# Output projection summed over three branches beside the DeltaNet, the input embedding inside the mixer, and three small edits

## The chip, the cores and the metric

The kernel runs on one core of a Trainium2 chip. The metric is the time of one execution on the device in microseconds (us); before the change it is 4006.65, the median of three runs (3999.32 to 4006.66). The engines are TensorE (PE, with PEld for its weight loads), VectorE (DVE), ScalarE (ACT), GpSimd (POOL) and SyncE (SP), which here issues every transfer.

## The reference

Two layers run over 512 positions of width 1024. Each layer: a norm, one input projection into four branches of 256 columns (retention A, a gated linear recurrence B, a diagonal state-space model C, a gated DeltaNet D), a norm of each branch, one output projection added to the residual h; then PEER (a top-k choice among 16384 single-neuron experts), added to h; then an embedding of the layer's own input p, times a gate, added to h.

```
def reference(x, p, positions, ...):
    h = x
    for l in range(DEPTH):                      # 2
        z = rmsnorm(h, mix_norm[l])
        (rq, rk, rv, rg, lg, lx, su, dqkv, db, da, dg) = jnp.split(z @ w_in[l], IN_SPLITS, axis=-1)
        y_ret, y_lru, y_s5, y_gdn = retention(...), rglru(...), s5(...), gated_deltanet(...)
        groups = (y_ret, y_lru, y_s5, y_gdn)
        mixed = jnp.concatenate([rmsnorm(y, branch_norm[l, j]) for j, y in enumerate(groups)], axis=-1)
        h = h + mixed @ w_out[l]
        h = h + peer(rmsnorm(h, ffn_norm[l]), peer_wq[l], peer_subkeys[l], peer_u[l], peer_v[l])
        gate = jax.nn.sigmoid(rmsnorm(h, ple_norm[l]) @ ple_wg[l])
        h = h + (p[l] @ ple_wp[l]) * gate
    return rmsnorm(h, final_norm)
```

## The kernel before

All of it is float32. The large products run as three matmuls of two parts each (`group3`): a tensor is split into a rounded high part (`split`: a cast on ACT) and the rest (a subtraction on DVE, or on POOL where `lo_eng` says so). Tokens lie in four blocks of 128 (`tb`), the 1024 columns of h in eight of 128 (`kd`).

In a layer, `mixer` streams `w_in` through `proj` and starts the DeltaNet D (`gen_D`) beside it; then, in the *middle* of the mixer, branches C, A and B run beside D. `self.mix` takes steps from several generators in turn by weights (RC, RA, ...); a scheduler sets from these steps, when the program is built, the fixed order of every engine, and each engine then works strictly in that order. PSUM is shared by banks: `bj` (tiles ps_j) for the branches, `bd` (ps_d) for D, `rbank` (ps_r) for the output projection.

D needs, for each of four token blocks and two pairs of heads, the inverse of two unit lower triangular matrices of 64x64 (`inverse`): a first level that POOL builds with a masked product (Tm) and the addition of the identity to X = (Tm, Mm), then five levels of two small matmul pairs, a masked product and a subtraction on DVE, and a transposition on PE copied back by ACT. Then `state` carries a state through the chunks: a chain of small matmuls and DVE steps, eight chunks long. `rsqrt` of 32 and 16 numbers per partition (drs for D, ars for A) is a power on POOL.

The finished branches lie in zm (a high and a low tile for each branch). `residual` is the output projection: `proj` over four blocks of 256 columns (tiles ps_r), of which the first two begin with the first six of the eight `kd` (`early=6`) while D runs. As each block of columns ends, DVE adds it to h, and `z_cols` prepares the norm that follows for the block before: four squares (zsq, ACT), and for each `kd` four transpositions (ps_t), zhi (ACT) and zlo (DVE). The next product, ps_q of PEER, reads zhi and zlo of all eight `kd`. h is loaded from memory (`open_h`, eight transfers on SP) into space that earlier tiles of the mixer hold till then.

`ple` is the gate stage: it loads p and ple_wp, splits them on ACT and POOL (tiles ph, pl, wph, wpl), and for each block of 256 columns and each `tb` takes 24 matmuls of the gate (ps_g), a tanh, six matmuls of the embedding (ps_q from wph, wpl) and two DVE steps into h. SP's queue is one for all: a transfer that has to wait holds up those behind it, such as the loads of s5t, which branch C reads. Line 347 is `mm`, 351 the subtraction of `split`, 344 `act`, 323 `rsqrt`, 335 `add`.

Of the kernel before, what the change touches and what calls it, by code (L numbers as in the profile page):

```python
# [12 lines left out]
I32 = mybir.dt.int32  # L13
# [53 lines left out]
def consts():  # L67
# [13 lines left out]
    f.add("nlv", -np.stack([lv[0], lv[0].T], 1).astype(np.float32))  # L81
    f.add("lvT", np.stack([m.T for m in lv[1:]], 1))
# [160 lines left out]
class Ker:  # L243
# [191 lines left out]
    def proj(self, z, wap, blocks, pool, bank, wmax=256, lo_eng=None, per=2, early=0):  # L435

# [30 lines left out]
        begun = {}  # L467
        if early:
            for i in range(2):
                for j in range(NTB):  # L470
                    n = blocks[i][1]
                    if i == 0:
                        begun[j] = bank()
                    ps = begun[j][:, i * n : (i + 1) * n]
                    zs = slice(j * P, (j + 1) * P)
                    for kd in range(early):
                        hi, lo = sp[2 * i + kd // 4]
                        zh, zl = z.at(kd)
                        self.group3(ps, zh[:, zs], zl[:, zs], hi[:, kd % 4, :n], lo[:, kd % 4, :n], kd == 0 and i == 0, False)
                    if j == NTB - 1:  # L480
                        for x in ((2, 3), (4,))[i]:
                            spl(x)
                    yield
        for j in begun:
            zs = slice(j * P, (j + 1) * P)
            for i in range(2):
                n = blocks[i][1]
                ps = begun[j][:, i * n : (i + 1) * n]
                for kd in range(early, KD):
                    hi, lo = sp[2 * i + kd // 4]  # L490
                    zh, zl = z.at(kd)
# [1480 lines left out]
```

## Time and profile before

| | |
|---|---|
| median of three runs | 4006.65 us |
| the profiled execution, on the device | 4006.07 us |
| its span, first to last instruction | 4004.0 us |
| mean granted clock of TensorE | 0.987 of full speed |
| PE, DVE, ACT, POOL busy | 97%, 72%, 38%, 16% |
| mixer, layer 0 (input projection, middle, output projection) | about 0 to 196, 196 to 300, 300 to 399 us |
| gate stage, layer 0 | about 1939 to 2020 us |
| mixer, layer 1 | about 2020 to 2196, 2196 to 2300, 2300 to 2368 us |
| gate stage, layer 1, and the last norm | about 3932 to 4004 us |

The rest, some 1500 us in each layer, is PEER. The times of stages are read from the first and the last instruction on their tiles. [...]

### The profile page before, as it was taken

The numbers are of one execution on the slowest core, as the hardware profiler recorded it, in microseconds if no ns is written. First come the engines' busy times: TensorE is split into PE (matmuls) and PEld (weight loads), VectorE is DVE, ScalarE is ACT, GpSimd is POOL, SyncE is SP. The second block draws the span as 40 slices with busy tenths as digits, with TensorE's granted clock in tenths as the row PEclk, the third lists the DMA queues.
The fourth block names the chain that finished last, engine by engine and source line by source line (L and its number), as shares of the span: only waits on it lengthen the run. The fifth ranks groups of instructions, "written<-read, shape, count | busy, mean of one in ns | idle before, by whom it ended". The sixth has DMA issues, their size and how long they took to land. (4 is left out here: it accounts for less than half of the span.)

```text
span 4004.0 us, 54147 instructions
## 1 busy us (share of the span) xinstructions
PE 3893.6 (97%) x20616; PEld 3231.0 (81%) x20616; DVE 2891.9 (72%) x5821; ACT 1512.0 (38%) x2173; POOL 621.5 (16%) x526
## 2 busy tenths in 40 slices
PE   7989999999999999999999899999899999999999
PEld 6768888878888888888898687777788888888888
DVE  9675899968888666555565769998588865555554
ACT  4344255652233233222443443566322232222223
POOL 4441000010002222222132310000100012222221
PEclk9989999999999999999999899999999999999999
DMA  4213254675653444333121133556756533333322
GB/s 146 83 29 106 75 200 176 241 268 187 202 169 122 139 137 150 124 118 109 48 99 45 41 122 110 188 203 244 238 182 201 160 110 127 112 120 118 124 79 85
DMA packets 306981, 554.06 MB, mean 138 GB/s; under 512 B 17696, under 2 KB 196000, under 8 KB 301344
## 3 DMA queue, kind: packets, MB, share of 16 engines
q1 hardware_dynamic: 306720, 550.60, 41.1%
q8 instruction: 162, 2.65, 0.3%
q14 instruction: 99, 0.81, 0.1%
HBM read 439.90 MB, written 110.63 MB: 137 GB/s over the span
## 5 line engine op out<-in xcount | busy, mean ns | idle before, releaser
L1670 DVE TENSOR_TENSOR h<-h,ps_v 128x512 f32<-128x512 f32 x1024 | 677.5, 681 | 627.5 <-PE ps_v L347 626.1
L347 PE MATMUL ps_v<-vhi,whi 128*128 128x512 f32 x2048 | 800.9, 391 | 20.7 <-ACT whi L350 20.3
L347 PE MATMUL ps_u<-zhi,ulo 128*128 128x512 f32 x2048 | 813.0, 397 | 0.5 <-DVE ulo L351 0.5
L347 PE MATMUL ps_u<-zhi,uhi 128*128 128x512 f32 x2048 | 809.9, 395 | 0.4 <-ACT aout L344 0.4
L347 PE MATMUL ps_u<-zlo,uhi 128*128 128x512 f32 x2048 | 808.2, 395 | 0.0
L347 PE MATMUL ps_v<-vlo,whi 128*128 128x512 f32 x2048 | 800.7, 391 | 0.0
L347 PE MATMUL ps_v<-vhi,wlo 128*128 128x512 f32 x2048 | 796.6, 389 | 0.0
L351 POOL TENSOR_TENSOR ulo<-uraw,uhi 128x1024 fp32r<-128x1024 f32 x136 | 328.7, 2417 | 2195.3 <-ACT uhi L350 1602.1
L350 ACT CAST uhi<-uraw 128x1024 fp32r<-128x1024 f32 x256 | 269.8, 1054 | 850.4 <-PE ps_u L347 572.0
L347 PEld LDWEIGHTS ps_v<-vhi,whi 128*128 128x128 f32 x2048 | 385.9, 188 | 104.7 <-ACT whi L350 21.2
L350 ACT CAST whi<-dact 128x512 fp32r<-128x512 f32 x256 | 158.5, 620 | 819.2 <-issue 378.7
L347 PEld LDWEIGHTS ps_u<-zhi,ulo 128*128 128x128 f32 x2048 | 384.9, 188 | 84.0 <-DVE ulo L351 1.4
L347 PEld LDWEIGHTS ps_u<-zlo,uhi 128*128 128x128 f32 x2048 | 385.0, 188 | 83.5
L347 PEld LDWEIGHTS ps_u<-zhi,uhi 128*128 128x128 f32 x2048 | 384.9, 188 | 82.9 <-ACT aout L344 1.2
L347 PEld LDWEIGHTS ps_v<-vlo,whi 128*128 128x128 f32 x2048 | 385.9, 188 | 81.2
L347 PEld LDWEIGHTS ps_v<-vhi,wlo 128*128 128x128 f32 x2048 | 385.2, 188 | 81.5
L332 DVE TENSOR_TENSOR dact<-dact,dg 128x512 f32<-128x512 f32 x256 | 320.6, 1256 | 34.5 <-ACT dact L344 17.1
L351 DVE TENSOR_TENSOR vlo<-vraw,vhi 128x1024 fp32r<-128x1024 f32 x256 | 311.5, 1235 | 26.0 <-ACT vhi L350 26.0
L344 ACT ACTIVATE tstg<-ps_g 128x512 f32<-128x512 f32 x256 | 264.3, 1157 | 128.3 <-PE ps_g L347 126.2
L350 ACT CAST vhi<-vraw 128x1024 fp32r<-128x1024 f32 x256 | 261.8, 1049 | 21.8 <-PE ps_v L347 20.2
L351 DVE TENSOR_TENSOR wlo<-dact,whi 128x512 fp32r<-128x512 f32 x256 | 180.8, 708 | 36.7 <-ACT whi L350 23.6
L329 DVE TENSOR_TENSOR to<-t_iota,tii 128x1024 f16<-128x1024 bf16 x256 | 172.0, 682 | 2.0 <-ACT tii L344 1.7
(467 smaller groups left out, 5410.3 us busy)
## 6 DMA issues: line engine op xcount, KB each, us to landing
uraw<-in_uT_dram SPq DMA_DIRECT2D x256, 512.0 KB, 3.5
vraw<-in_v_dram SPq DMA_DIRECT2D x256, 512.0 KB, 3.8
Gd<-tstg SPq DMA_DIRECT2D x32, 2048.0 KB, 7.0
dg<-Gd SPq DMA_DIRECT2D x64, 1024.0 KB, 6.0
Ad<-aout SPq DMA_DIRECT2D x120, 256.0 KB, 2.1
dact<-Ad SPq DMA_DIRECT2D x120, 256.0 KB, 3.4
wraw<-in_w_in_dram SPq DMA_DIRECT2D x40, 512.0 KB, 3.5
wraw<-in_w_out_dram SPq DMA_DIRECT2D x16, 512.0 KB, 3.6
```

The costliest lines, as they stand in the source:

```text
L329: (eng or self.V).tensor_tensor(out, a, b, op=op)
L332: (eng or self.V).tensor_tensor(out, a, b, op=ALU.mult)
L344: self.A.activation(out, x, f, **k)
L347: self.PE.matmul(out, l, r, start=start, stop=stop)
L350: self.A.copy(hi, x)
L351: (lo_eng or self.V).tensor_tensor(lo, x, hi.bitcast(F32), op=ALU.subtract)
L1670: self.reached = V.tensor_tensor(self.h[:, tb, ds], self.h[:, tb, ds], ps, op=ALU.add).ins
```

## The change

1. Output projection. `residual` goes; `out_early` sums, for two halves of 512 columns, the products of the three branches A, B and C (kd 0 to 5), taken in steps beside D (weight RE = 3). The first half goes to SBUF (`part`, four ACT copies), the second stays in PSUM (`held`). `out_late`, after D, adds `part` to h, then D's two kd to each half and token block, adds each to h, and calls `z_cols` once the last token block of a half is done. So 768 matmuls of 256 columns become 384 of 512.
2. Embedding. p @ ple_wp is no longer computed in `ple`, but in `gen_embed`, taken beside C, A, B and D (weight RA). Its splits go to ACT and DVE; the product is written to memory (Pd) and read back as emb by `ple`. pT and ple_wp pass through the buffer ak of branch A.
3. Residual. The pools of the mixer are laid out in another sequence, and some small tiles of D and A go into another pool, so that the space of h is free sooner.
4. Small edits: `rsqrt` of 16 or more numbers on DVE (a first guess and three Newton steps, ten operations); the first level of `inverse` without POOL's product and addition, as a DVE subtraction and one more transposition (`turned`); the factor lam as two ACT operations in place of one on POOL.

```diff
 def rsqrt(self, pool, out, x, n, tag):
-        self.G.tensor_tensor(out, x, self.mhalf.to_broadcast([P, n]), op=ALU.pow)
+        V = self.V
+        if n < 16:
+            self.G.tensor_tensor(out, x, self.mhalf.to_broadcast([P, n]), op=ALU.pow)
+            return
+        y = out
+        t = pool.tile([P, n], F32, name="rsq_t", tag=tag + "t")
+        V.tensor_scalar(y.bitcast(I32), x.bitcast(I32), -0.5, 1597463007.0, op0=ALU.mult, op1=ALU.add)
+        for _ in range(3):
+            V.tensor_tensor(t, y, y, op=ALU.mult)
+            V.scalar_tensor_tensor(t, t, -0.5, x, op0=ALU.mult, op1=ALU.mult)
+            V.scalar_tensor_tensor(y, t, 1.5, y, op0=ALU.add, op1=ALU.mult)
...
         def inverse(tb, hp):
-            self.mul(lam, m2(low), la2, G)
+            for h in range(2):
+                self.act(lam[:, h], low, AF.Copy, scale=la[:, tb, 2 * hp + h : 2 * hp + h + 1])
...
-            self.mul(Tm, Lm, m2(c("nlv")[:, 0]), G)
...
-            self.mul(Mm, h2(ps[:, 0:256]), m2(c("nlv")[:, 1]))
+            AT = pool.tile([P, 2, P], F32, name="dAT", tag="dAT", bufs=4)
+            self.mul(AT, h2(ps[:, 0:256]), m2(c("lvT")[:, 0]))
             self.mul(aT, h2(ps[:, 256:512]), m2(c("tri")))
-            self.add(X, X, self.ident.unsqueeze(1).unsqueeze(1).to_broadcast([P, 2, 2, P]), G)
+            self.sub(Mm, m2(self.ident), AT)
+            yield
+            def turned():
+                ps = bank()
+                for h in range(2):
+                    self.PE.transpose(ps[:, h * P : (h + 1) * P], Mm[:, h, :], self.ident)
+                self.act(fl(Tm), ps[:, 0:256], AF.Copy)
+            turned()
...
 def mixer(...):
-            self.a_alloc(mx)
             self.b_alloc(mx)
             self.c_alloc(mx)
+            self.mix_alloc(mx)
+            self.d_alloc(mx)
+            self.a_alloc(mx)
...
-                self.mix([(upto(C, "c_half"), self.RC), (a_(), self.RA), (b_(), self.RA), (upto(D, "d_half"), 1)])
+                W = self.gen_embed(l, self.pool(c1, "em", sa), bj, Pd)
+                self.mix([(upto(C, "c_half"), self.RC), (a_(), self.RA), (b_(), self.RA), (W, self.RA), (upto(D, "d_half"), 1)])
...
-            pj = self.residual(self.zm, self.ap["w_out"][l], wp)
+            pj = self.out_early(self.zm, self.ap["w_out"][l], wp)
...
-                self.take(pj, 8)
+                self.mix([(pj, self.RE), (D, 1)])
                 drain((D, 1))
...
-                self.blockwise(pj, znew, gain, banks(...), wp, 0)
+                self.out_late(self.zm, znew, gain, banks(...), wp)
...
+    def out_early(self, z, wap, pool):
...
+        for hf in range(2):
+            b = [self.rbank() for _ in range(NTB)]
+            for c in range(3):
+                spl(3 * hf + c + 1)
...
+                for tb in range(NTB):
+                    self.out_mm(z, b[tb], hf, c, tb, c == 0, hf == 0 and c == 2)
+                    yield
+            if hf == 0:
+                for tb in range(NTB):
+                    self.act(self.part[:, tb, :], b[tb], AF.Copy)
+        self.held = b
...
+    def out_mm(self, z, ps, hf, c, tb, first, last):
+        hi, lo = self.late_w[hf, c]
+        ts = slice(tb * P, (tb + 1) * P)
+        for k in range(2):
+            zh, zl = z.at(2 * c + k)
+            self.group3(ps, zh[:, ts], zl[:, ts], hi[:, k], lo[:, k], first and k == 0, last and k == 1)
+    def out_late(self, z, znew, gain, bank, pool):
...
+            self.add(hs, hs, self.part[:, tb, :])
+        for tbs in ((0, 1, 2), (3,)):
+            for hf in (1, 0):
+                for tb in tbs:
+                    ps = self.held[tb] if hf else self.rbank()
+                    self.out_mm(z, ps, hf, 3, tb, hf == 0, True)
+                    hs = self.h[:, tb, cs[hf]]
+                    self.add(hs, hs, ps)
+                if tbs == (3,):
+                    for i in (2 * hf, 2 * hf + 1):
+                        self.z_cols(znew, gain, i, bank, pool)
...
+    def gen_embed(self, l, pool, bank, Pd):
...
+        nc.sync.dma_start(praw, self.ap["pT"][l].rearrange("(k p) t -> p k t", p=P))
+        parts = [self.zm.at(6 + k) for k in range(2)]
+        for k in range(2):
+            self.split(*parts[k], praw[:, k])
...
+        for i in range(4):
+            wh, wl = (pool.tile([P, 2, 256], F32R, name=n, tag=n) for n in ("wph", "wpl"))
+            self.split(wh, wl, raw(i))
+            load(i + 2)
...
+                        self.group3(ps[:, o : o + 256], ph[:, ts], pl[:, ts], wh[:, k], wl[:, k], k == 0, k == 1)
+                e = self.av[:, t0 : t0 + 2, :]
+                self.act(fl(e), ps, AF.Copy)
+                nc.sync.dma_start(Pd[:, t0 : t0 + 2, 256 * i : 256 * i + 256], e)
...
 def ple(...):
-                    p2 = bq()
-                    for k in range(2):
-                        self.group3(p2[:, 0:256], ph[:, k, ts], pl[:, k, ts], wh[:, k, cs], wl[:, k, cs], k == 0, k == 1)
-                    self.stt(tg, tg, 1.0, p2[:, 0:256], ALU.add, ALU.mult)
+                    self.stt(tg, tg, 1.0, emb[i][:, tb], ALU.add, ALU.mult)
...
-            self.split(ph, pl, praw, self.G)
-            self.split(wh, wl, wraw, self.G)
```

Places in the engines' fixed order. PE, layer 0, middle of the mixer, before: aq and sx are transposed for branches A and C, s5t and xb are products of C and B, ps_d is D.

```order
L347 MATMUL ps_d<-dX,cb 128x256
L1032 MATMUL ps_j<-ca,aq 128x128 x2
L347 MATMUL ps_d<-dX,cb 128x256
L1032 MATMUL ps_j<-ca,aq 128x128
L347 MATMUL ps_j<-s5t_2296,sx_2322 128x256
L1032 MATMUL ps_j<-ca,aq 128x128 x4
L347 MATMUL ps_j<-xb,lruw 128x512
L347 MATMUL ps_d<-dX,cb 128x256 x2
L347 MATMUL ps_d<-dS,dwT 64x128
L347 MATMUL ps_d<-dkT 128x128 x2
```

The same place after; wph, wpl and zm are the parts of ple_wp and of p.

```order
L687 MATMUL ps_d<-ca,dX 128x128 x2
L360 MATMUL ps_d<-dX,dE 128x128 x2
L360 MATMUL ps_d<-dAT,dX 128x128 x4
L1015 MATMUL ps_j<-ca,aq 128x128
L360 MATMUL ps_j<-wph,zm_2433 128x256
L360 MATMUL ps_j<-wpl,zm_2433 128x256
L360 MATMUL ps_j<-wph,zm_2434 128x256
...
L1241 MATMUL ps_j<-ca,sx_2343 128x128
L1015 MATMUL ps_j<-ca,aq 128x128
L1241 MATMUL ps_j<-ca,sx_2343 128x128
L360 MATMUL ps_d<-dAT,dX 128x128 x2
```

Blocks of twelve matmuls of the embedding now stand between those of D and the branches.

SP, layer 0, at the end of the input projection, before: Td is the prepared state space of branch C, s5t its reload.

```order
L448 DMA wraw<-in_w_in_dram 128x4x256 x2
L1095 DMA Td_65<-s5p_1027 128x2048
L448 DMA wraw<-in_w_in_dram 128x4x256 x5
L1062 DMA s5t_2297<-Td_65 128x2560
L1062 DMA s5t_2299<-Td_65 128x1024
L1062 DMA s5t_2301<-Td_65 128x2048
L1062 DMA s5t_2303<-Td_65 128x8
L1067 DMA s5t_2296<-Td_65 32x4x512 x4
L1221 DMA gluw<-in_glu_w_dram 128x2x512
```

After:

```order
L1078 DMA Td_65<-s5p_1022 128x2048
L460 DMA wraw<-in_w_in_dram 128x4x256
L1905 DMA ak<-in_pT_dram 128x2x512
L1916 DMA ak<-in_ple_wp_dram 128x2x256
L1045 DMA s5t_2315<-Td_65 128x2560
L1045 DMA s5t_2317<-Td_65 128x1024
L1045 DMA s5t_2319<-Td_65 128x2048
L1045 DMA s5t_2321<-Td_65 128x8
L1050 DMA s5t_2314<-Td_65 32x4x512 x4
L1204 DMA gluw<-in_glu_w_dram 128x2x512
L937 DMA lruw<-in_lru_w_dram 128x512
L1916 DMA ak<-in_ple_wp_dram 128x2x256 x2
```

pT and a first part of ple_wp have moved ahead of s5t; the second uses the buffer that the first has left.

PE, layer 0, end of the output projection, before (zm is D's and the other branches' parts; ps_t is a transposition of h):

```order
L347 MATMUL ps_r<-whi,zm_3105 128x256
L347 MATMUL ps_r<-wlo,zm_3105 128x256
L347 MATMUL ps_r<-whi,zm_3106 128x256
L364 MATMUL ps_t<-ca,h 128x128 x8
L347 MATMUL ps_q<-zhi,whi 128x512
L347 MATMUL ps_q<-zlo,whi 128x512
L347 MATMUL ps_q<-zhi,wlo 128x512
```

After:

```order
L360 MATMUL ps_r<-whi,zm_2433 128x512
L360 MATMUL ps_r<-wlo,zm_2433 128x512
L360 MATMUL ps_r<-whi,zm_2434 128x512
L377 MATMUL ps_t<-ca,h 128x128 x4
...
L360 MATMUL ps_r<-whi,zm_2433 128x512
L360 MATMUL ps_r<-wlo,zm_2433 128x512
L360 MATMUL ps_r<-whi,zm_2434 128x512
L377 MATMUL ps_t<-ca,h 128x128 x16
L360 MATMUL ps_q<-zhi,whi 128x512 x4
L377 MATMUL ps_t<-ca,h 128x128 x4
L360 MATMUL ps_q<-zlo,whi 128x512
L360 MATMUL ps_q<-zhi,wlo 128x512
```

Before, eight transpositions lie between the last ps_r and ps_q; now sixteen stand between the last ps_r and the first ps_q, and eight more among the first ps_q.

ACT, layer 0, behind D's last piece of zm, before:

```order
L344 ACTIVATE zm_3105<-ps_d,gv 128x128 x2
L344 ACTIVATE zsq,zss<-h 128x256
L350 CAST whi<-wraw 128x1024
L344 ACTIVATE zsq,zss<-h 128x256
L350 CAST whi<-wraw 128x1024
L344 ACTIVATE zsq,zss<-h 128x256 x6
L344 ACTIVATE zhi<-ps_t,gv 128x512 x2
L350 CAST whi<-wraw 128x1024
L344 ACTIVATE zsq,zss<-h 128x256
L350 CAST whi<-wraw 128x1024
L344 ACTIVATE zsq,zss<-h 128x256
```

After:

```order
L357 ACTIVATE zm_2433<-ps_d,gv 128x128 x2
L357 ACTIVATE zsq,zss<-h 128x256 x5
L363 CAST whi<-wraw 128x1024
L357 ACTIVATE zsq,zss<-h 128x256
L363 CAST whi<-wraw 128x1024
L357 ACTIVATE zsq,zss<-h 128x256
L357 ACTIVATE zhi<-ps_t,gv 128x512 x2
L357 ACTIVATE zsq,zss<-h 128x256 x3
L363 CAST whi<-wraw 128x1024
L357 ACTIVATE zsq,zss<-h 128x256
L357 ACTIVATE zhi<-ps_t,gv 128x512
L357 ACTIVATE zsq,zss<-h 128x256
```

The items are the same in kind; in the new order sixteen zsq and eight zhi follow D's last piece with 30 ps_r on PE beside them, where 204 of half the width were beside them before.

## Rows read from the trace of the kernel before

**Rows 1.** The page, first section: engines' busy time, share of span, instructions.
```profile
PE 3893.6 (97%) x20616; PEld 3231.0 (81%) x20616; DVE 2891.9 (72%) x5821; ACT 1512.0 (38%) x2173; POOL 621.5 (16%) x526
```

**Rows 2.** The chain that ended last: start us, us, engine, tile, line, matmuls.
```profile
2359.80 8.27 PE ps_r L347 x69
2382.98 31.73 PE ps_q L347 x136
3272.23 5.48 PE ps_v L347 x24
3969.05 4.19 PE ps_g L347 x35
```

**Rows 3.** Stretches of both mixers: length, engines' busy us, PEclk, DMA share, GB/s.
```profile
196.00:282.00 86.00, 66.11 (x358) 54.55 (x359) 66.17 (x126) 38.00 (x83) 40.28 (x31) 0.80 0.14 40
2196.00:2275.00 79.00, 59.99 (x325) 48.07 (x324) 67.89 (x127) 37.01 (x73) 38.01 (x32) 0.85 0.20 61
240.00:260.00 20.00, 11.35 (x58) 9.62 (x58) 20.00 (x26) 5.06 (x6) 15.70 (x11) 0.70 0.00 1
```

**Rows 4.** PE in layer 0, by time: start, us, line, tiles, [idle before <-releaser].
```profile
192.13 1.95 PE L347 MATMUL ps_d<-dAT,dX 128*128 128x128 f32 x16
202.32 3.62 PE L347 MATMUL ps_d<-dAT,dX 128*128 128x128 f32 x16
250.76 1.22 PE L347 MATMUL ps_d<-dkT 64*128 64x128 f32 x4 [7.37 <-DVE dE L332]
```

**Rows 5.** Instructions by line and form: count, busy us, mean ns, idle before.
```profile
L347 PE MATMUL ps_q<-wph,ph 128*128 128x256 f32 x64 | 18.0, 284 | 0.0
L323 POOL TENSOR_TENSOR drs<-dss,mhalf 128x32 f32<-128x32 f32 x2 | 11.0, 5476 | 1.7 <-DVE dss L638 1.7
L335 POOL TENSOR_TENSOR dX<-dX,ca 128x512 f32<-128x512 f32 x16 | 20.9, 1325 | 4.6 <-DVE dX L332 3.2 <-DVE daT L332 1.3
L351 DVE TENSOR_TENSOR wlo<-dact,whi 128x512 fp32r<-128x512 f32 x256 | 180.8, 708 | 36.7 <-ACT whi L350 23.6 <-PE ps_v L347 2.5
```

**Rows 6.** The gate's start in both layers, by time: start us, us, engine, line.
```profile
1947.90 4.54 POOL L351 TENSOR_TENSOR wpl<-wpraw,wph 128x2048 fp32r<-128x2048 f32 x1
1947.97 4.50 DVE L412 TENSOR_SCALAR zrsh<-zrs 128x4 f32<-128x4 f32 x1 [0.54 <-POOL zrs L323]
3940.06 0.17 DVE L412 TENSOR_SCALAR zrsh<-zrs 128x4 f32<-128x4 f32 x1 [0.40 <-POOL zrs L323]
```

**Rows 7.** Stretches of the gate's start, columns as in rows 3.
```profile
1950.00:1955.00 5.00, 1.55 (x13) 1.56 (x14) 4.19 (x6) 0.69 (x1) 2.44 (x1) 0.98 0.01 3
1955.00:1960.00 5.00, 5.00 (x32) 5.00 (x32) 2.50 (x3) 2.32 (x3) 0.00 (x0) 0.68 0.14 46
3935.00:3940.00 5.00, 4.09 (x32) 3.64 (x31) 3.85 (x5) 3.87 (x6) 0.98 (x1) 1.00 0.31 104
```

**Rows 8.** Stretches of the output projection, columns as in rows 3.
```profile
340.00:372.00 32.00, 28.13 (x192) 21.95 (x190) 16.33 (x54) 10.67 (x31) 5.51 (x10) 0.98 0.11 37
372.00:400.00 28.00, 27.96 (x226) 27.78 (x227) 18.94 (x31) 18.85 (x47) 1.37 (x8) 0.96 0.74 259
2320.00:2380.00 60.00, 59.10 (x437) 54.50 (x436) 32.49 (x67) 27.84 (x67) 10.59 (x52) 1.00 0.46 150
```

**Rows 9.** Behind the output projection, by line and form; columns as in rows 5.
```profile
L344 ACT ACTIVATE zhi<-ps_t,gv 128x512 fp32r<-128x512 f32 x40 | 26.2, 685 | 21.1 <-PE ps_t L364 21.1
L344 ACT ACTIVATE zsq<-h 128x256 f32<-128x256 f32 x48 | 20.0, 417 | 27.9 <-DVE h L341 13.0 <-DVE h L335 12.6 <-ACT zsq L344 1.1
L344 ACT ACTIVATION_READ_ACCUMULATOR zsq<-h 128x1 f32 x48 | 9.1, 189 | 0.0
L350 ACT CAST whi<-wraw 128x1024 fp32r<-128x1024 f32 x88 | 91.7, 1045 | 109.4 <-PE ps_j L347 29.7 <-PE ps_q L347 29.2 <-DMA wraw<-in_w_in_dram 12.7
L335 DVE TENSOR_TENSOR h<-h,ps_r 128x256 f32<-128x256 f32 x32 | 12.6, 416 | 13.7 <-PE ps_r L347 11.1 <-DMA h<-in_x_dram 2.0 <-DMA h<-Hd 0.3
```

**Rows 10.** One issue of the DMA list: KB each, median us to landing.
```profile
praw<-in_pT_dram SPq DMA_DIRECT2D x2, 512.0 KB, 3.9
```

More of the change, by code (lines that the diff above doesn't have):

```diff
@@ L611, in gen_D @@
         yield
[L612 removed]
+        S = self.dS
         V.memset(S, 0.0)
@@ L851, in a_alloc @@
         self.ag = pool.tile([P, NTB, 256], F32, name="ag")
+        self.am = [pool.tile([P, 4, 32], F32, name="am%d" % i) for i in range(2)]
     def a_cons(self, what):
@@ L1828, in take, with load, spl @@
             next(g, None)
-    def residual(self, z, wap, pool):
-        def cons(i):
-            def f(tb, ps):
-                hs = self.h[:, tb, 256 * i : 256 * i + 256]
-                self.add(hs, hs, ps[:, 0:256])
-            return f
-        return self.proj(z, wap, [(256 * i, 256, "T", cons(i)) for i in range(4)], pool, lambda: self.rbank(), per=4, early=6)
+    def out_early(self, z, wap, pool):
+        nc = self.nc
+        seq = [(0, 0), (0, 1), (0, 2), (1, 0), (1, 1), (1, 2), (0, 3), (1, 3)]
+        raws, w = {}, {}
+        self.part = pool.tile([P, NTB, 512], F32, name="part")
+        def load(x):
+            if x < len(seq):
+                hf, c = seq[x]
+                raws[x] = pool.tile([P, 2, 512], F32, name="wraw", tag="wraw", bufs=2)
+                nc.sync.dma_start(raws[x], wap[256 * c : 256 * c + 256, 512 * hf : 512 * hf + 512].rearrange("(k p) c -> p k c", p=P))
+        def spl(x):
+            if x < len(seq):
+                hf, c = seq[x]
+                tag = lambda n: dict(name=n, tag=n if c < 3 else n + str(hf), bufs=2 if c < 3 else 1)
+                w[hf, c] = [pool.tile([P, 2, 512], F32R, **tag(n)) for n in ("whi", "wlo")]
+                self.split(*w[hf, c], raws.pop(x))
+                load(x + 2)
+        load(0)
+        load(1)
+        yield
+        spl(0)
+        yield
+        self.late_w = w
+        for hf in range(2):
+            b = [self.rbank() for _ in range(NTB)]
+            for c in range(3):
+                spl(3 * hf + c + 1)
+                if c == 2 and hf == 1:
+                    spl(7)
+                for tb in range(NTB):
+                    self.out_mm(z, b[tb], hf, c, tb, c == 0, hf == 0 and c == 2)
+                    yield
+            if hf == 0:
+                for tb in range(NTB):
+                    self.act(self.part[:, tb, :], b[tb], AF.Copy)
+        self.held = b
+        yield
@@ L1937, in run @@
             last = l == L - 1
-            self.ple(l, zs[a], None if last else zs[b], None if last else self.gain("mixg", l + 1), out)
+            self.ple(l, zs[a], None if last else zs[b], None if last else self.gain("mixg", l + 1), out, Pd)
             if not last:
```

135 lines of the change are left out of this document (62 added, 73 removed).

## The prediction

> **What bounds the kernel now.** The first section of the page says that TensorE (PE) is busy for 97% of the span [rows 1], and the chain of waits is nearly all matmuls. So a microsecond counts if it takes matmuls off a stretch where PE is full, or puts matmuls where PE stands idle. The chain gives the prices. A matmul of 256 columns takes 4.19 / 35 = 0.120 us (gate, ps_g) and 8.27 / 69 = 0.120 (output projection, ps_r). One of 512 columns takes 5.48 / 24 = 0.228 to 31.73 / 136 = 0.233 us [rows 2]. The table of stretches then shows where PE is not full: in both mixers, in the stage where the branches A, B, C and the DeltaNet D run side by side. [...] Sixteen small matmuls of an inverse take 1.95 us at 192 us and 3.62 at 202, the two levels of the clock, and one wait of 7.37 us there is for DVE [rows 4]. From 240 to 260 us DVE has no free time and PE works 11.35 of 20 us [rows 3]. The output projection and the gate are otherwise full: 27.96 of 28 us in layer 0's last stretch [rows 8].
>
> **The change, part by part.** The sum is made against the profiled execution, 4006.07 us (span 4004.0 and 2.07 around it; the median of the runs is 4006.65).
>
> 1. Embedding. The gate stage loses 3 x 64 = 192 matmuls of 256 columns [rows 5], which stand in a full PE: 192 x 0.120 = **-23.0**.
>
> 2. Start of the gate. In layer 0 GpSimd (POOL) subtracts wpl for 4.54 us, and the DVE's tiny zrsh (128x4), started beside it, takes 4.50 us; in layer 1, where no such subtraction runs, it takes 0.17 [rows 6]. PE then works 1.55 of 5 us and has a mean clock of 0.68 in the next five [rows 7]: 3.45 + 5 x 0.32 = 5.0 lost. The subtraction leaves POOL, so -5.0. [...] In layer 1 PE already loses 0.9 us there [rows 7], and embedding matmuls no longer fill that start: 0 to +2, I take +1. Together **-4**.
>
> 3. Wider output projection. 768 x 0.120 = 92.1 us become 384 of 512 columns: 87.7 at 0.228, 89.6 at 0.233, so -2.5 to -4.4; I take **-3.4**. [...] Running it beside D is only a move: PE is idle there for 3.9 us (340 to 372) and 0.9 us (2320 to 2380) [rows 8], so 0 to -4.8. I take 0, because in the new order layer 0's last two steps of D still have only six of its matmuls each.
>
> 4. Inverse of D. 32 more transposes: 32 x 1.95 / 16 = 3.9 us on PE, [rows 4] for the price of such a 128-column instruction. In the chain of one inverse POOL's add of 1.33 us [rows 5] goes; a DVE subtraction of 128x256 (0.42 [rows 9]), two transposes (0.24) and a copy on ACT come. That is about even. 0 to +4, I take **+1**.
>
> 5. Roots. POOL's power for drs takes 5.48 us twice [rows 5]; ten small DVE steps at 0.17 us, the price of the small row in [rows 6], take 1.7. D starts up to 3.8 us earlier per layer, but PE is full of in-projection meanwhile. 0 to -7, I take **-2**.
>
> 6. Embedding in the mixer. The 192 matmuls need 23 us at full clock, 46 at half, and find 38.9 us of idle PE [rows 3]. DVE gets, per layer, six splits of 128x512 (0.708), four subtractions of 0.42 and ten small steps: 4.2 + 1.7 + 1.7 = 7.6 us, 15.2 for both, and has 19.8 + 11.1 us free, though not between 240 and 260 us. A third of the 15.2 on the path: I take **+5**. The ends are 0 (all hidden) and +46 (each matmul at half clock ahead of one that the chain waits for). I am near the low end because that long PE wait there is for DVE [rows 4].
>
> 7. SP's queue. In layer 0 the load of ple_wp stands ahead of s5t, and it waits until pT has landed (3.9 us [rows 10]) and has been split (two casts and two subtractions, some 2 us). Everything behind it on SP, s5t and gluw, waits too, and branch C waits for s5t; D doesn't. 0 to +6, I take **+1.5**.
>
> 8. The end of the output projection. Before, h's columns are finished block by block, and PE still has ps_r while ACT and DVE make the next norm's zsq, zhi, zlo: nothing is exposed [rows 8]. Now all columns become final together. In layer 0 PE has, after the last piece of D, 30 matmuls of 512 columns and 24 transposes: 7.0 + 2.9 = 9.9 us. ACT has, in its order ahead of the first zhi that ps_q reads, fifteen squares (0.417 + 0.189), three casts (1.045) and, with that zhi, five zhi (0.685) [rows 9]: 9.1 + 3.1 + 3.4 = 15.6, beginning after three DVE adds (about 0.7 each, by the 128x512 row of [rows 5]): 17.7. PE stands for 7.8 us. In layer 1, 56 matmuls are left: 13.1 + 2.9 = 16.0; the first add comes after 32 of them (7.5), then 14 squares, one cast and five zhi (12.9): 20.4, so 4.4 idle. With a little for the lower clock after it: **+13**. Ends: 0, if ACT gets ahead, and +22 (each gap 3 us longer, and the clock as in [rows 7]).
>
> 9. Residual loads. DVE's adds waited 2.0 + 0.3 us for h [rows 9]; PE had matmuls meanwhile: 0 to -2.3, I take **-1**.
>
> Sum: -23 - 4 - 3.4 + 1 - 2 + 5 + 1.5 + 13 - 1 = -12.9. 4006.07 - 12.9 = **3993**.
>
> **The rivals.**
> - DVE is the bound of the mixer's middle. For it: 240 to 260 us, and the 7.37 us wait. Then all 15.2 us of new DVE work lie on the path, the transposes cost 4 and the late s5t 6: 10.2 + 3 + 4.5 more than I took, 4011, no change that can be seen. Against: POOL gives up 20.9 us of adds there [rows 5], and DVE is slowed beside POOL.
> - Slower: the embedding matmuls stand in PE's queue in front of matmuls that D's chain waits for, while the clock is low. At half clock they are 46 us. From 26 of them on the path (5 as taken and 21 more) the whole is over 0.2% slower; at three quarters, 34.5, it is 4023. Against: 38.9 us idle.
> - Everything is hidden and ACT gets ahead at the end: terms 4, 6, 7 and 8 are 0, 20.5 less: 3973. For it: DVE and ACT have free time on average. Against: ACT's order counted in 8.
> - The filled idle time brings the clock back. At 1.0 in place of 0.80 and 0.85 PE's busy time in the two stretches would fall by 66.1 x 0.20 + 60.0 x 0.15 = 22 us; where DVE sets the pace this is worth nothing, at half it is 11 us: 3982. [...]
> - The move doesn't do what it says: D ends later by as much as is put beside it. Then 8 stays and 3 is only the narrower sum; that is what I took.
>
> **How the numbers follow.** Forecast 3993, with its own range 3984 to 4002: 0.60. Everything hidden 0.12, clock back 0.05, DVE the bound 0.16, slower 0.07. About 0.2% (8 us) is what a measurement of this kernel can tell from no change. Below 3998.6: most of the forecast's range (0.51), the two better cases 0.17 and a little of DVE's: 0.70. Above 4014.7: the slower case and a tail: 0.08. Between: 0.22. The range for 8 in 10 leaves out half of the hidden case below and the slower case with part of DVE's above: 3970 to 4008.
>
> **What would show it.** Term 1: the gate stages with ps_g alone, each some 11.5 us shorter. 2: zrsh at 0.17 in layer 0. 6: the length of the stage of [rows 3], with PE busier and its clock; if it grows by over 10 us a layer with DVE full, the first rival holds, with PE full at a low clock the second. 7: the start of the s5t loads. 8: PE's idle time between the last ps_r and the first ps_q, and ACT without a gap in it; if it is gone, the third. 9: no DMA wait ahead of h's adds. I am wrong above all if 6 or 8 is mis-sized.

## The result: slower by half a per cent, and the profile after

The changed kernel takes 4025.76 us (median of 5, 4022.56 to 4029.23); the kernel before, run beside it, 4005.37 (3999.32 to 4006.66). The ratio is 1.0052, 95% interval 1.0039 to 1.0066. The forecast was 3993 with a range up to 4008. The profiled run of the changed kernel took 4022.56 us, its span is 4020.9.

The span can be cut at the starts of the first and last matmuls of each stage. Lengths are in us; layer 1 is counted from the last ps_g of layer 0. The last two columns are two of the experiments below (three repairs; the same with the old output projection). Each column is one profiled execution. The kernel before alone took between 3999.32 and 4008.99 us in its executions, so a difference of a few us in a single stretch proves little.

| stretch (layer 0 / layer 1) | before | after | repaired | repaired, old projection |
|---|---|---|---|---|
| to the last in-projection | 191.5 / 185.4 | 198.6 / 185.0 | 189.1 / 185.0 | 189.5 / 183.4 |
| from there to the last s5t x sZ (mixer) | 94.4 / 81.4 | 98.1 / 86.4 | 92.4 / 88.0 | 92.5 / 87.4 |
| to the last ps_r (output projection) | 112.7 / 90.5 | 110.1 / 84.5 | 114.9 / 82.6 | 111.7 / 84.8 |
| to the last ps_q of the expert stage (its first in brackets) | 45.3 (1.0) / 46.5 (1.0) | 54.4 (7.4) / 63.1 (10.3) | 52.6 (5.7) / 54.0 (4.2) | 45.3 (1.0) / 46.6 (1.0) |
| to the last ps_v (experts) | 1494.6 / 1517.3 | 1494.3 / 1518.3 | 1495.0 / 1513.9 | 1494.2 / 1516.5 |
| to the last ps_g (gate; its first in brackets) | 72.0 (3.2) / 62.9 (4.2) | 62.5 (9.5) / 56.6 (5.5) | 54.9 (3.2) / 53.6 (4.2) | 55.1 (3.2) / 56.4 (4.2) |

The gates became 15.8 us shorter, not 27. Layer 0's in-projection became 7.1 longer, the ends of the output projections 9.1 and 16.6 (forecast 13 in all). TensorE has fewer matmuls than before, 20264 for 20616 [rows 1], and is busy for 8.5 us longer, 3902.1 for 3893.6; page of after, first section:

```profile
PE 3902.1 (97%) x20264; PEld 3214.6 (80%) x20264; DVE 2907.4 (72%) x5881; ACT 1533.1 (38%) x2248; POOL 550.3 (14%) x470
```

**Layer 0's in-projection.** Stretches of the kernel before (columns as in [rows 3]; PEclk is the mean granted clock of TensorE as a share of full speed), and the same of after:

```profile
20.00:40.00 20.00, 17.61 (x84) 14.14 (x82) 18.67 (x57) 9.42 (x14) 6.19 (x5) 1.00 0.30 86
140.00:160.00 20.00, 17.57 (x95) 13.62 (x93) 15.44 (x34) 7.45 (x9) 13.88 (x12) 1.00 0.00 0
```

```profile
20.00:40.00 20.00, 17.62 (x84) 14.52 (x83) 12.63 (x17) 6.87 (x8) 9.38 (x6) 0.98 0.44 126
140.00:160.00 20.00, 14.57 (x80) 12.79 (x78) 13.04 (x39) 7.28 (x17) 5.68 (x5) 0.83 0.00 0
160.00:180.00 20.00, 14.85 (x85) 10.49 (x85) 12.69 (x39) 7.62 (x13) 13.36 (x20) 0.83 0.00 1
```

DVE misses 6 us of work between 20 and 40 us, and PE works 3 us less from 140 on at a mean clock of 0.83. The missing work is the preparation of the S5 matrix, whose input s5raw is loaded at 37 us instead of 10; its DVE work then stands ahead of the DeltaNet's, and ACT waits for dla with everything behind it. The load's row in the list by tile (first and last start), of before and of after, and then ACT by time, of after:

```profile
L1084 SPq DMA_DIRECT2D s5raw<-in_s5vec_dram x2: 328/379/430, 10.4 to 868.6; - x2
```

```profile
L1067 SPq DMA_DIRECT2D s5raw<-in_s5vec_dram x2: 340/382/423, 37.2 to 885.5; - x2
```

```profile
146.88 2.44 ACT L357 ACTIVATE dX<-cb,dla 128x128 f32<-128x128 f32 x8 [7.07 <-DVE dla L354]
```

**Layer 0's gate.** By time, of after: SP, ACT, PE, then two stretches.

```profile
1955.68 1.21 SPq L1949 DMA_DIRECT2D emb<-Pd  x2
1956.98 1.78 SPq L460 DMA_DIRECT2D wraw<-in_ple_wg_dram  x2
...
1963.91 1.04 ACT L363 CAST whi<-wraw 128x1024 fp32r<-128x1024 f32 x1 [1.43 <-DMA wraw<-in_ple_wg_dram]
...
1965.01 1.23 PE L360 MATMUL ps_g<-whi,zhi 128*128 128x256 f32 x4 [0.58 <-ACT whi L363]
```

```profile
1960.00:1965.00 5.00, 3.03 (x14) 1.85 (x12) 2.20 (x8) 3.52 (x7) 1.01 (x1) 0.58 1.04 343
1965.00:1970.00 5.00, 4.95 (x21) 4.66 (x22) 3.76 (x4) 2.21 (x3) 0.00 (x0) 0.50 0.52 158
```

The gate's first weights leave when the experts' last matmuls are done, at 1957 us. In the kernel before they left at 1552:

```profile
1552.24 0.93 SPq L448 DMA_DIRECT2D wraw<-in_ple_wg_dram  x2
```

PE works 3.03 of the five us from 1960 on at a mean clock of 0.58, and in the next five the clock is 0.50: from 1966.65 to 1969.86 us a matmul of 256 columns starts every 0.214 us, where the full PE of the kernel before took 0.120 for one [rows 2]. In the kernel before the clock is 1.00 over the sixteen matmuls of 1.95 us at 192 us and 0.50 over those of 3.62 at 202 [rows 4].

**Layer 1's end of the output projection.** By time, of after:

```profile
2374.31 0.21 POOL L1355 MEMSET t_start<- 128x128 bf16 x1 [18.25 <-PE ps_r L360]
...
2376.42 5.14 DVE L1359 CAST t_iota<-ca 128x256 bf16<-128x256 f32 x1
...
2381.20 0.21 POOL L1357 MEMSET t_row<- 128x128 bf16 x1
2381.48 1.39 DVE L354 SCALAR_TENSOR_TENSOR zlo<-ps_t,gv,zhi 128x512 fp32r<-128x512 f32 x2
2382.27 1.97 PE L377 MATMUL ps_t<-ca,h 128*128 128x128 f32 x8 [5.65 <-DVE zlo L354]
```

A small cast lasts 5.14 us, until GpSimd's 48 memsets are over; zlo and PE wait for it. In layer 0 of after, where no memset runs beside it, it takes 0.28. But memsets alone don't decide: the same cast of the kernel before stands in the same kind of stream and takes 0.35, and there the memset begun after it takes 0.34 where those around it take 0.20. By time, of before:

```profile
2368.45 0.35 DVE L1376 CAST t_iota<-ca 128x256 bf16<-128x256 f32 x1
...
2368.60 0.34 POOL L1374 MEMSET t_row<- 128x128 bf16 x1
```

In before the cast starts with the fifth memset, in after amid the stream, behind the fifteenth. What makes the difference, these traces don't show.

### The profile page after: what moved, and what is told of

Its sections match the earlier page's. It is cut to its first block, busy times and chain, and to the rows that moved or that the text cites. A ratio compares the mean times of both kernels' runs of the same rounds, so it can differ in the third digit from the quotient of the medians.

```text
span 4020.9 us, 53500 instructions
## 1 busy us (share of the span) xinstructions
PE 3902.1 (97%) x20264; PEld 3214.6 (80%) x20264; DVE 2907.4 (72%) x5881; ACT 1533.1 (38%) x2248; POOL 550.3 (14%) x470
## 4 chain that ended last, share of the span: by engine, by line
PE 86%; DVE 6%; ACT 1%; DMA 1%; issue 1%; POOL 0%; SPq 0%; DVEq 0%; POOLq 0%; ACTq 0%
PE ps_v L360 34%; PE ps_u L360 33%; PE ps_g L360 5%; PE ps_j L360 4%; PE ps_d L360 3%; PE ps_q L360 2%; PE ps_r L360 2%; PE ps_s L360 1%; DMA wraw<-in_ple_wg_dram 0%; DVE ulo L364 0%; PE ps_d L687 0%; DVE wlo L364 0%; PE ps_t L377 0%; DMA Gd<-tstg 0%; DVE tk_tmp L1343 0%
## 5 line engine op out<-in xcount | busy, mean ns | idle before, releaser
L360 PEld LDWEIGHTS ps_v<-vlo,whi 128*128 128x128 f32 x2048 | 385.8, 188 | 81.4
```

What stands on the lines that cost most here:

```text
L360: self.PE.matmul(out, l, r, start=start, stop=stop)
```

## The experiments

Each kernel ran five times or more beside the kernel before, whose median was 4005.19 to 4006.16. The first group undoes one suspect each in the changed kernel.

**e1_pad: the gate's pool back in its place**
```diff
             sp = self.pool(c, "ls")
+            sp.tile([P, 6144], F32, name="lspad")
             wp = self.pool(c, "lw")
```


> The changed kernel with one unused tile of 24 KB per partition in front of the gate's weight pool, so that this pool lies again where it lay in the kernel before, clear of the buffers that the expert stage still uses. Theory (a smaller pool moved the gate's weights onto space that comes free late): the first load of ple_wg leaves at about 1550 us instead of 1957 in layer 0 and at about 3920 instead of 3944 in layer 1; the stretch from the last ps_v to the first ps_g falls from 9.5 to about 3.5 us in layer 0 and from 5.5 to about 4 in layer 1, and the time falls by 6 to 9 us, to 4017 to 4020. Rival (the loads are not what the gate's start waits for; PE waits there for ACT's zhi anyway): the loads are early and the time stays within 2 us of 4025.8.

Measured 4012.78, ratio to before 1.0016 (1.0007 to 1.0025): 13.0 less than after and below the range expected. Layer 0's first load of ple_wg leaves at 1571 us and its first ps_g comes 3.5 us after the last ps_v, at once after ACT's zhi:

```profile
1961.24 0.58 PE L360 MATMUL ps_g<-whi,zhi 128*128 128x256 f32 x1 [2.22 <-ACT zhi L357]
```

The gates give 5.8 + 2.9; another 4.0 come from layer 1's expert stage, which takes 1513 to 1518 us over all these kernels, for a reason I did not find.

**e2_layout: the mixer's buffers in their old pools and order**
```diff
-            self.b_alloc(mx); self.c_alloc(mx); self.mix_alloc(mx); self.d_alloc(mx); self.a_alloc(mx)
+            self.a_alloc(mx); self.b_alloc(mx); self.c_alloc(mx)
...  (cb, vec, rsin, rcos, dS, dsc, dvb, am where they were)
```


> The changed kernel with the mixer's buffers allocated in the old order and places (cb, vec, rsin, rcos, dS, dsc, dvb and am as in the kernel before); everything else of the change stays. Theory (the new places make the load of s5raw wait for the normalisation's released buffers, so that the preparation of the layer's S5 matrix starts late, DVE's work piles up, and the DeltaNet's first steps come late): s5raw is issued at about 10 us again instead of 37, DVE works 18 instead of 12.6 of the 20 us from 20 on, layer 0's in-projection ends 5 to 8 us earlier, at 191 to 194 instead of 198.6, and the time is 4017 to 4021. Rival (the late start of D comes from lam on ACT and the added roots on DVE, not from the places): the load is early, the in-projection still ends after 197, and the time is above 4023.

Measured 4014.35, 1.0020 (1.0011 to 1.0029): 11.4 less, again below the range expected. The in-projection ends at 190.2, which is 8.4 of it; what is left comes behind it in layer 0. Stretches of this kernel:

```profile
20.00:40.00 20.00, 17.44 (x81) 13.93 (x80) 18.38 (x56) 9.03 (x13) 6.40 (x5) 0.98 0.27 81
140.00:160.00 20.00, 17.93 (x96) 14.37 (x96) 17.59 (x45) 6.92 (x8) 11.21 (x13) 0.97 0.00 0
```

lam is still on ACT here and the roots on DVE, so the rival is out.

**e4_iota: one cast from DVE to ACT**
```diff
-self.V.tensor_copy(self.t_iota, ...)
+self.A.copy(self.t_iota, ...)
```


> The changed kernel with one instruction moved: the cast of the 128x256 index row t_iota, which DVE does at the end of the output projection ahead of the next norm's zlo, is done by ACT. Theory (in layer 1 this cast stood for 5.14 us beside GpSimd's 48 memsets and held zlo back, and the clock fell behind it): PE's wait of 5.65 us for zlo goes to at most 1 us, the clock stays up in 2380 to 2400, layer 1's stretch from the last ps_r to the first ps_q falls from 10.3 to some 5 us, and the time falls by 5 to 9 us to 4017 to 4021. Rival (DVE's next instruction is held by the memsets in its place, or ACT becomes late with the cast): the wait stays within 2 us of what it was and so does the time.

Measured 4018.01, 1.0030 (1.0019 to 1.0041): 7.8 less. By time, in this kernel:

```profile
2376.53 0.40 ACT L1359 CAST t_iota<-ca 128x256 bf16<-128x256 f32 x1
...
2378.73 2.11 PE L377 MATMUL ps_t<-ca,h 128*128 128x128 f32 x8 [0.91 <-DVE zlo L354]
```

**x_all: the three together ("repaired" in the table)**

> The three edits together on the changed kernel: the unused tile in front of the gate's weights, the old places of the mixer's buffers, the cast of t_iota on ACT. Theory (three side effects of places and one shared stretch cost the gain): they lie in different stages and add up to 16 to 26 us, so 4000 to 4010, about the kernel before or a little under. Rival (what was paid is the embedding's matmuls in the mixer at a low clock, as the slower case of the prediction had it): undoing the three gives under 8 us, the time stays above 4018, and the stage of the four branches is the one that is longer than before by 10 us or more in a layer.

Measured 3986.55, 0.9946 (0.9933 to 0.9960): 39.2 less than after, where 16 to 26 were expected and the three alone gave 32.2. All three causes stand, and the rival falls. Why they give 7.0 more together than alone is not shown.

**b_pk: the kernel before, with only s5raw's place shifted**
```diff
-prep(self.pool(c2, "pk", sb), bd)
+pk = self.pool(c2, "pk", sb); pk.tile([P, 1632], F32, name="pkpad"); prep(pk, bd)
```


> The kernel before with nothing of the change, but with one unused tile of 6.4 KB per partition ahead of the buffers of the S5 preparation, so that s5raw lies as far towards the normalisation's buffers as it does in the changed kernel. Theory (the place of s5raw alone costs layer 0's start): s5raw leaves at about 37 us instead of 10, DVE works under 14 instead of 18.7 of the 20 us from 20 on, layer 0's in-projection ends 4 to 9 us later than 191.5 and the time is 4009 to 4015. Rival (it needed lam on ACT or the roots on DVE as well): the load is late, but the in-projection ends within 2 us of 191.5 and the time is under 4008.

Measured 4011.13, 1.0014 (1.0005 to 1.0023): 5.9 more. This shows the mechanism without the change: s5raw leaves at 36.0, the in-projection ends 10.6 later, of which the mixer gives 3.6 back. What the trace shows is the mechanism in layer 0; the price in the time is half of that in e2_layout.

```profile
20.00:40.00 20.00, 17.62 (x84) 14.53 (x83) 12.59 (x17) 6.82 (x7) 9.31 (x6) 0.98 0.43 137
```

**y_mid: new order, old size of the pool**

> The three edits together, except that the mixer's buffers keep the new order (B's and C's first, A's last) and only dS, dsc, dvb and two of am go back to the pools they lay in before, so that the mixer's pool is as large as before. Theory (the size of this pool, not the order in it, moved s5raw): s5raw leaves at about 10 us, the in-projection ends at 189 to 191, and the time is within 4 us of 3986.6; if the order is what lets h's loads go early, they leave at about 350 us and DVE no longer waits 2.8 and 5.3 us for h, worth up to 4 us. Rival (the order matters for s5raw too): it leaves at 37 us and the time is 3995 or more.

Measured 3986.02, 0.9952 (0.9938 to 0.9965), as the repaired kernel; s5raw leaves at 10.2. So it was the pool's size. The hope for h's loads missed: they leave at 380.5, late again. Early residual loads and an early s5raw excluded each other in the places tried.

The second group prices the terms of the forecast, by undoing one part in the repaired kernel (3986.55).

**y_noemb: embedding in the gate as before**

> The changed kernel with the mixer's buffers in their old places and t_iota's cast on ACT (as in the run of the three edits together), but with the embedding in the gate stage as in the kernel before, its pool and all. The gate terms and the embedding's cost in the mixer are what this run tells. Theory (terms 1, 2 and 6 as forecast): both gate stages are longer by 27 us together (72 and 63 us again), the stretches from the in-projection to the last s5t x sZ are shorter by 3 to 8 us together, and the time is 3986.6 + 19 to 24, about 4006 to 4011. Rival (the embedding's matmuls in the mixer cost nothing, since idle TensorE takes them): the mixer stretches stay within 1 us and the time is 4012 to 4014; other rival (they cost 10 us or more): 4003 or less.

Measured 4003.76, 0.9994 (0.9985 to 1.0003): the move is worth 17.2, less than the 19 to 24 expected. The gates are 25.0 longer without it, so everything else together pays 7.8 for it. The mixers, to the last s5t x sZ, are 6.0 and 10.5 shorter without it, also more than expected; but half of that comes back behind that mark, 5.3 of it in layer 1's stretch from the last ps_r to the last ps_q.

**y_1mm, y_nodve: what the embedding costs in the mixer**
```diff
-self.group3(ps, ph, pl, wh, wl, ...)
+self.mm(ps, ph, wh, ...)              # y_1mm
+self.group3(ps, ph, ph, wh, wh, ...)  # y_nodve, no subtractions on DVE
```


> The three edits together, with one of three of the embedding's matmuls left: only high part by high part, 64 in place of 192 (the embedding is then only as precise as that). Its splits, copies and transfers stay. Against the run without the embedding in the mixer, its 192 matmuls, splits and transfers there cost 16.5 us (6.0 and 10.5 in the two stretches to the last s5t x sZ). Theory (TensorE pays: PE has no idle time that these matmuls could take without delaying D's chain or the branches): two thirds go, the time is 3974 to 3979. Rival (VectorE pays: the splits stand in front of D's and C's steps): within 3 us of 3986.6.

> The three edits together, with all of the embedding's 192 matmuls, but without VectorE's six subtractions per layer for them (the high parts stand in for the low ones, so the embedding is not computed to full precision). Theory (TensorE pays): within 3 us of 3986.6. Rival (VectorE pays, the term's 15.2 us of VectorE work lie on the path): 3974 to 3981.

y_1mm: 3977.15, 0.9927 (0.9914 to 0.9941), 9.4 less. y_nodve: 3999.33, 0.9982 (0.9973 to 0.9991). The first fits TensorE as the payer; nothing shows VectorE's subtractions as the price. But y_nodve (it leaves out the low parts and multiplies the high ones three times) was expected to stay where it was and came out 12.8 longer, most of it in four stretches (+3.8 in layer 0's mixer; in layer 1 -2.9 in the mixer, +3.5 to the last ps_r, +5.2 from there to the last ps_q). I take it for another order of the scheduled instructions, and have not shown it. If that is so, a new order alone can move this kernel by as much as most single differences below, and none of them is a clean price.

**y_oldout: old output projection and residual**

> The three edits together, and besides the output projection and residual of the kernel before (256-column matmuls, h finished block by block). Theory (terms 3 and 8 as forecast: 3.4 us gained by wide matmuls, 13 or more lost because the next norm starts when all is finished): the stretches from the last ps_r to the last ps_q are 45 to 48 us again instead of 52.6 and 54.0, about 14 us shorter together, the stretches of ps_r itself are 3 to 8 longer, and the time is 3986.6 - 6 to 11, 3975 to 3981. Rival (the early columns beside the DeltaNet's chain are worth what the end costs): the time is 3985 or more.

Measured 3974.75, 0.9922 (0.9909 to 0.9936), the fastest of all. By time, PE at the end of layer 0's projection in the repaired kernel, and in this one:

```profile
400.56 0.65 PE L373 MATMUL ps_t<-ca,h 128*128 128x128 f32 x4 [1.65 <-DVE zlo L350]
401.38 0.66 PE L373 MATMUL ps_t<-ca,h 128*128 128x128 f32 x4 [0.17 <-DVE zlo L350]
402.10 1.74 PE L356 MATMUL ps_q<-zhi,whi 128*128 128x512 f32 x4
```

```profile
393.78 1.11 PE L373 MATMUL ps_t<-ca,h 128*128 128x128 f32 x8
394.65 0.48 PE L356 MATMUL ps_q<-zhi,whi 128*128 128x512 f32 x1
```

With the old order PE goes on without a wait. The two ends are 14.7 shorter; mixer and ps_r together are only 1.5 shorter, and layer 1's gate is 2.8 longer. So the wide projection, as a whole, costs 11.8 us here. With the embedding left in the gate (y_noemb against z_oldout_noemb below) it costs 5.6.

**z_oldout_noemb: that, and the embedding in the gate**

> The three edits together, with the old output projection and the old place of the embedding, so that of the change the inverse, the roots and the small pieces stay. Against the run with the old output projection and the embedding moved (3974.75), it prices the moved embedding alone. Theory (gate 25 us gained, mixer 16 us paid): 3982 to 3987. Rival (the 17 us of the earlier comparison hold): 3990 to 3994.

Measured 3998.19, 0.9982 (0.9973 to 0.9991): 23.4 more than y_oldout, above both ranges. The gates account for 24.6, so the embedding in the mixer costs 1.2 net here, not 16: the mixers are 17.6 shorter without it to the last s5t x sZ, and 17.0 longer from there to the last ps_r (11.9 of it in layer 0). The mark is a step of branch C, and D goes on behind it. Also, what is left of the change here, the inverse, the roots and the small pieces, is only 7.2 below the kernel before. Stretches of this kernel:

```profile
320.00:340.00 20.00, 18.39 (x125) 14.53 (x124) 7.08 (x21) 5.45 (x17) 2.97 (x5) 0.97 0.08 26
340.00:360.00 20.00, 19.96 (x80) 14.44 (x78) 8.80 (x30) 5.55 (x17) 2.51 (x5) 0.50 0.01 2
```

PE has work for 19.96 of 20 us, and its granted clock is 0.50, behind a stretch in which it worked 18.39. With the embedding moved (y_oldout) both stretches show 1.00; the second of them:

```profile
340.00:360.00 20.00, 19.21 (x136) 14.77 (x134) 13.29 (x44) 7.99 (x23) 3.90 (x8) 1.00 0.08 27
```

**y_rsq: roots on GpSimd as before**

> The three edits together, with the inverse roots by GpSimd's power as in the kernel before. It measures the term that was forecast at -2 us. Theory (the in-projection of layer 0, which ended 2.4 us earlier with the three edits than before, owes this to the roots): 3988 to 3991, nearly all of it ahead of the end of layer 0's in-projection. Rival (the roots are hidden): within 1.5 us of 3986.6.

Measured 3992.28, 0.9967 (0.9955 to 0.9979): the roots are worth 5.7, of which 1.9 ahead of the end of the in-projection, where nearly all was expected, and 3.9 in layer 0's mixer.

**y_inv, z_add, z_lam: the old inverse, and its two pieces**

> The three edits together, with the inverse of the DeltaNet as in the kernel before (lam, the first level's mask and the added identity on GpSimd, one pair of transposes less). It measures the term that was forecast at +1 us. Theory from the run without the embedding, whose mixer stretches were 8.0 and 3.9 us shorter than before without it (the new inverse gains, because it takes slow GpSimd work out of D's chain): the stretches from the in-projection to the last s5t x sZ grow by 5 to 12 us together and the time is 3991 to 3998. Rival (the term as forecast, the gain lies elsewhere): 3984 to 3988.

> The three edits together, with the first level of the inverse as before (mask and added identity on GpSimd, no pair of transposes), lam staying on ACT. Theory (these two steps, 0.9 and 1.39 us each time and up to 19 us of GpSimd's time per layer, stand between E and the first level's matmuls): 12 to 18 us of the 20, 3998 to 4005, and GpSimd's busy time from 240 to 280 us is above 20 us instead of 13. Rival (lam brought it): under 3990.

> The three edits together, with lam of the inverse on GpSimd again, and nothing else undone. Theory (every GpSimd step in an inverse's chain costs its own length and what it waits behind GpSimd's work for branch C): lam is one of three such steps and the first of its inverse, where there is most slack: 2 to 6 us, 3988 to 3993. Rival (lam alone is the gain of 20 us): 4000 or more.

y_inv (all of it): 4006.91, 1.0003 (0.9994 to 1.0012), 20.4 more. z_add (first level's mask and identity on GpSimd): 4010.83, 1.0015 (1.0006 to 1.0024), 24.3 more. z_lam: 3994.44, 0.9973 (0.9962 to 0.9983), 7.9 more. All three missed upwards. The pieces don't add up, but the first level carries it. Three engines of z_add in layer 0, rows picked in order of time:

```profile
262.98 1.83 POOL L342 TENSOR_TENSOR sZ<-s5t,zm 128x508 f32<-128x508 f32 x1 [1.16 <-DVE zm L1245]
263.01 0.67 DVE L342 TENSOR_TENSOR sZ<-s5t,zm 128x508 f32<-128x508 f32 x1
264.78 1.70 POOL L345 TENSOR_TENSOR dX<-dX,ca 128x512 f32<-128x512 f32 x1
265.30 1.73 DVE L342 TENSOR_TENSOR sx<-s5t,zm 128x508 f32<-128x508 f32 x1
266.95 0.41 DVE L342 TENSOR_TENSOR dX<-ps_d,cb 128x256 f32<-128x256 f32 x1
267.51 1.26 POOL L345 TENSOR_TENSOR dX<-dX,ca 128x512 f32<-128x512 f32 x1 [1.02 <-DVE dX L342]
267.84 0.66 PE L357 MATMUL ps_d<-dS,dkT 128*64 128x128 f32 x2 [2.89 <-DVE daT L342]
269.80 3.44 POOL L345 TENSOR_TENSOR dX<-dX,ca 128x512 f32<-128x512 f32 x2 [1.03 <-DVE dX L342]
270.24 0.41 DVE L342 TENSOR_TENSOR daT<-ps_d,cb 128x256 f32<-128x256 f32 x1
271.86 1.50 PE L357 MATMUL ps_d<-dX,dE 128*128 128x128 f32 x12
```

```profile
260.00:280.00 20.00, 11.19 (x66) 9.07 (x65) 18.19 (x31) 5.47 (x8) 10.02 (x7) 0.83 0.06 21
```

The same stretch of the repaired kernel:

```profile
260.00:280.00 20.00, 19.41 (x125) 16.65 (x124) 16.18 (x33) 9.31 (x16) 0.00 (x0) 0.94 0.11 39
```

The first level waits for four adds, one behind another on GpSimd and each between two steps on other engines, while PE works 11.19 of 20 us. Beside GpSimd's work DVE's products are not all of one length: sx, begun 0.52 us after an add of GpSimd, takes 1.73 us, where a like one at 263.01, begun 0.03 us after a product of GpSimd, takes 0.67 and GpSimd's beside it 1.83 (the shortest of its form takes 1.26). Why the lengths differ, these traces don't show.

**z_slow: the embedding at half the rate**

> The three edits with the old output projection, and the embedding taken at half the rate among the branches (0.2 instead of 0.4 of a piece per piece of D), so that its matmuls reach further towards the end of the stage. Theory (the embedding's matmuls cost TensorE's time wherever the stage is nearly full of matmuls, so the density matters little): within 4 us of 3974.75. Rival (they cost because they stand packed in front of what D and C wait for): 3964 to 3970.

Measured 3977.03 (3972.74 to 3987.34), 0.9934 (0.9921 to 0.9948): no clear difference from y_oldout, and not the rival's gain. Density is not what it costs.

## Why the prediction was wrong

The step that failed first is one that the sum didn't have: the buffers' new places. The diff moves buffers between pools and shrinks the gate's pool, and the prediction took from that only term 9, the loads of h that come earlier. It never asked what else would lie over space that comes free late. Both s5raw and ple_wg do. e2_layout and e1_pad price this at 11.4 and 13.0 us (4 of which may not belong to it). The second failed step is term 8 in layer 1, which had no cast of 5.14 us on DVE ahead of zlo: 7.8 (e4_iota). Without the three the change gives 18.6 us, and the forecast's 12.9 would have been near.

That nearness is partly luck. The prices below come from undoing one part at a time, and they don't add up: all terms together would give about -33 (-26.4 for 1 and 2, +11.8 for 3 and 8, -20.4 for 4, -5.7 for 5, +7.8 for 6 and 7), where the repaired kernel is 18.6 below the kernel before. A price holds beside the other parts only.

1. Embedding out of the gate and 2, its start: forecast -27. From the last ps_v to the last ps_g, the repaired kernel shows -17.1 and -9.3 = -26.4. Right in size; zrsh takes 0.17 us, as [rows 6] had it for layer 1. In the change itself 10.6 of it were lost; early weights give back 8.7 of these (e1_pad).
3. Wider projection: -3.4 forecast. y_oldout shows nothing of it: with the wide projection mixer and ps_r together are 1.5 longer.
4. Inverse: +1 forecast, -20 measured in the repaired kernel. This is the worst-sized term. I counted the add's 1.33 us against what replaced it and called it about even. I left out the masked product Tm and the factor lam, which also leave GpSimd; of before, 100 to 300 us:

```profile
L332 POOL TENSOR_TENSOR dX<-dE,cb 128x256 f32<-128x256 f32 x8 | 8.5, 1074 | 6.0 <-DVE dE L332 6.0
L332 POOL TENSOR_TENSOR dX<-cb,dla 128x256 f32<-128x256 f32 x8 | 6.8, 864 | 21.2 <-DVE dla L341 15.4 <-PE ps_d L347 4.9 <-issue 0.8
```

   And I didn't count that the adds queue on one engine with branch C's products, that the first level waits for four of them, and that a product on DVE takes 1.73 us beside such an add (0.67 at 263.01 in z_add). But the 20 isn't the inverse's worth by itself: in z_oldout_noemb the inverse, the roots and the small pieces together give 7.2, with the clock at 0.50 for a stretch; and a part of the 20 can be order, as in y_nodve.
5. Roots: -2 forecast, -5.7 measured, inside its ends.
6. Embedding in the mixer: +5 forecast; 7.8 net with the wide projection, 1.2 with the old one, so right in size. The 16.5 to the last s5t x sZ is not its price, since the stretches behind that mark get shorter by half of it (wide projection) or nearly all of it (old one). I chose the low end because a long PE wait was for DVE, and that reason is not borne out: removing two thirds of the matmuls gave 9.4, removing DVE's subtractions no gain. The DVE sum was also short: the new inverse has eight subtractions of 128x256 in a layer, not four, 1.7 us more.
7. SP's queue: +1.5 forecast, not tested by itself. The first s5t load leaves 3.6 us behind the last in-projection matmul (before, 1.6 us ahead of it), and in the repaired kernel PE waits 1.3 us for it.
8. End of the projection: +13 forecast; +14.8 in the repaired kernel. The mechanism is in part as forecast: in layer 0 ACT is busy for 5.00 of the 5 us from 395 to 400, but PE's waits for zlo are 2.6 and 1.2 us, not 7.8 and 4.4. The lower clock (0.75 from 400 to 405 us) and the transpositions that now stand behind the last ps_r take part in the rest; their shares are not measured. In the change itself it was 25.7, since layer 1's part was mis-sized: my count of ACT's steps had no DVE instruction of 5.14 us ahead of zlo. Terms 3 and 8 together, +9.6, compare with the 11.8 of y_oldout.
9. Residual loads: in after no add waits for them; with the old places DVE waits 2.8 + 5.3 us. No run had the early loads and the repairs together, so their worth stays open.

Of the rivals, none is what happened. The slower one (embedding at half clock) gave nearly the right time, 4023, for a wrong reason: with the places and the cast repaired, and the embedding still in the mixer, the kernel is 0.5% faster than before. Its 46 us at half clock, an end of term 6 too, counts 0.240 for a matmul; after shows 0.214 at a clock of 0.50, or 41 us for 192. "DVE bound" is not borne out: all the new DVE work is in the repaired kernel, and y_nodve, without a part of it, is not faster. "The clock comes back" is partly borne out: the granted clock from 260 to 280 us is 0.61 before, 0.83 in y_noemb and 0.94 in the repaired kernel, and from 340 to 360 us it is 0.50 in z_oldout_noemb and 1.00 in y_oldout. That filled idle time is what brings the clock back is not shown: the 0.50 in z_oldout_noemb stands behind a stretch in which PE worked 18.39 of 20 us. The higher clock may be how the embedding's matmuls pay for themselves there; no run separates it.

## What to carry to other kernels

A diff that moves or resizes buffers moves loads: for each pool that changes, list what comes to lie over it, who frees that space last, and when the load left before. Price an instruction on a shared engine by the queue it stands in and by who waits for it, not by its own length against its replacement's. If a change comes out slower than its parts promise, undo side effects one by one before blaming the main idea: here three small ones hid 39 us, and one of the intended parts (the wide projection) cost 12 more. To price a part that has moved, take the whole time, not the stretch that it moved into: the mark that ends the stretch can move with it.

## What the runs showed of the hardware that I had not expected

- In after a DVE cast of 128x256 stayed 5.14 us in flight beside 48 GpSimd memsets of 0.21 us each, started 0.15 us apart, and ended 0.15 us behind the last of them; in e1_pad it took 4.47 and in e2_layout 5.26, and without them 0.28. So a row of 48 short GpSimd instructions stood beside a DVE instruction about as long as the one of 4.50 us beside a single GpSimd instruction of 4.54 in the kernel before [rows 6]. It need not: in the kernel before the same cast took 0.35 beside the memsets.
- Two DVE instructions that read PSUM took 0.41 us each beside GpSimd's adds (at 269.91 and 270.24 in z_add), as one at 269.24 did with GpSimd idle; the product of two SBUF operands took 1.73 beside an add and 0.67 at 263.01.
- In z_oldout_noemb TensorE was busy for 19.96 of 20 us with a granted clock of 0.50, behind a stretch of 18.39. The full PE row with few matmuls (80, where y_oldout has 136 in the same stretch at 1.00) was a slow PE.
